# Memory keys and values from float32 weights as loaded, and no convolution chunk on TensorE

## The chip, the cores and the metric

One core of a Trainium2 chip runs the whole program. The metric is device time in microseconds (us) of one execution. Engines are called as the profile calls them: PE (TensorE; PEld is its weight load), DVE (VectorE), ACT (ScalarE), POOL (GpSimd), SP (SyncE, whose queue issues nearly all DMAs here). Each engine takes its instructions in an order that the program's scheduler fixed when the kernel was built.

## What is computed

One decoding step of a two-layer decoder for 512 prompt tokens and 64 sample tokens (8 sequences of 8), model width 1024. Layer 0 mixes tokens with a conformer convolution, layer 1 with causal pooling; each layer then has cross-attention into 256 memory tokens and a gated feed-forward part. The parts that the change touches:

```python
def _mem_kv(mem, g_mem, w_kv):          # for each layer: mem [256, 1024], w_kv [1024, 2048]
    kv = (_rmsnorm(mem, g_mem) @ w_kv).reshape(b, N_MEM, 2, N_MEM_HEADS, MEM_HEAD_DIM)
    return kv[:, :, 0], kv[:, :, 1]

def _conformer_conv(h, prefix, ...):
    u = h @ w_in + b_in                 # [1024, 2048]
    a, gate = jnp.split(u, 2, axis=-1)
    glu = a * jax.nn.sigmoid(gate)
    c = _causal_dwconv(concat(prefix, glu), w_dw, b_dw)      # 31 taps, each channel by itself
    c = silu(layernorm(c, ln_g, ln_b))
    return c @ w_out + b_out
```

The keys and values of the memory are outputs, and the attention of their layer reads them. All products are wanted in float32 precision.

## The kernel before, in words

**Products.** A float32 product is made of three float16 products: both operands are split into hi and lo halves (`cp`, L137, on ACT writes hi; `lo`, L140, on DVE writes the rest), and hi·hi, hi·lo and lo·hi are added in PSUM by `mm` (L130). Turning goes through `tr` (L134), a PE transpose.

**Weight stream.** `build_units` lists all weights in the order of use, as units of 1 MB. SP loads each half (512 KB, L217 in `emit_dma`) into one of three raw buffers; `convert_next` splits the half into a slot (8 KB a partition; there are nine). `pump(n)` starts up to n further units if a slot is free; `get` starts units until the one asked for is there; `drop` frees a slot. A slot goes to the unit that was written next in the program, first freed first used, and the unit's conversion waits until the slot's earlier content has been read.

**Layer 0's mixer** (`conv_module`). Eight `pair(p)` steps, one for each 128 channels, multiply the normed tokens by `a_w_in` (24 products of 512 columns and 24 of 64 for each of gate and value); ACT evaluates them (L766 to L769), DVE multiplies (L770, L771). The 31-tap convolution of a chunk of channels follows as soon as its pair is done, with a lowered priority: by `PLAN`, chunks 0 and 2 (after pair 2), 4 (after pair 4), 5 and 6 (after pair 7) run on DVE as 31 steps each that add into PSUM (L657, L661); chunks 1 and 3 run on ACT (products) and POOL (sums, L676); chunk 7 runs on PE (`conv_pe`) as 93 products with diagonal matrices that `diag_build` makes on POOL (L725). The convolution of the sample tokens is shared by DVE (L689), ACT and POOL (`prefix_s`, `fresh_s`). Results lie in `CT`.

**Memory keys and values.** `mem_load` loads the 256 memory tokens. For each layer `mem_norm` normalises them (with the layer's gain row, a broadcast DMA, L280) and `mem_turn` turns and splits them, in pairs 2 to 4. `kv_part(l, n)`, eight in all, then multiplies them by a [1024, 512] piece of `c_w_kv`, which is two units: 2 x 24 products of 512 columns, evaluated by ACT and written out twice by SP (L594 to the output, L596 to a scratch from which attention loads them). After each part `pump(2)` starts two units. Units of layer 1's parts 1 to 3 are held back until convolution chunk 6 is done (`after`, L225).

**Then** the layer norm of the convolution (`ln_a`: PE turns, statistics on DVE L855, result on ACT L860; `ln_b`: turn back, ACT L874, split), first for token tiles 0 and 1, interleaved with the last parts; then the product with `a_w_out` (`natural_stage`), which in program order comes after all eight parts; then attention.

Of the kernel before, what the change touches and what calls it, by code (L numbers as in the profile page):

```python
# [14 lines left out]
D = 1024  # L15
# [31 lines left out]
class Step:  # L47
    """The whole inference step. On-chip data live in one SBUF tile cut by hand; the products are exact
    16-bit splits (hi + lo) of both operands, scaled by powers of two, accumulated in float32."""

    def __init__(self, tc, ctx, ins, outs):
# [25 lines left out]
        self.PA0 = take(288)  # L77
# [7 lines left out]
        self.after = {}  # L85
        self.free = deque(range(self.NSLOT))
# [7 lines left out]
    # ---- views  # L94
# [29 lines left out]
    def release(self, s):  # L124
        if s < 100:
            self.free.append(s)

    # ---- engine helpers
# [13 lines left out]
    # ---- weight stream  # L142
    def build_units(self):
# [60 lines left out]
        self.rawat = {}  # L204
        self.special = {("down", 0): None}

    def emit_dma(self, upto):
        while self.n_dma < min(upto, 2 * len(self.units)):
            u, half = divmod(self.n_dma, 2)
            r = self.rawq()  # L210
            src = self.units[u][1][half]
            dst = self.f(self.RAW0 + r * 1024, 1024)
# [5 lines left out]
            self.rawat[self.n_dma] = r  # L218
# [38 lines left out]
    def pump(self, n=1):  # L257
        while n > 0 and self.n_cv < len(self.units):
            key = self.units[self.n_cv][0]
            if not self.free and not (self.lent and key[0] in ("K", "V") and key[2] in self.lent_to):  # L260
# [14 lines left out]
    # ---- norms  # L275
# [29 lines left out]
    def split_T(self, h0, P, hi, lo):  # L305
        """h0 [P tokens, 1024] -> hi/lo views [128, 8, P] of its transpose."""
# [9 lines left out]
    def split_D(self, src, o, dst):  # L316
        """src [128 tokens, 1024] -> hi/lo views [128, 8, 128] of its transpose, turned on the way by the DMA."""
# [57 lines left out]
    def nat_prompt(self, acc, act, woff, nk, hook=None):  # L375
        """acc [128, 1024] = act^T . 64 w;  act(k, s) the stationary [128, 128]."""
# [14 lines left out]
    def nat_last(self, acc, act, woff, nk, half):  # L391
        """nat_prompt by halves of the output's columns, with half(n) after each."""
# [10 lines left out]
    def nat_sample(self, acc, act, woff, nk, order=None, hooks=None):  # L403
        """acc rows 0..63: hi part, rows 64..127: lo part of the 64 sample tokens."""
# [12 lines left out]
    def fold(self, acc, tmp, out):  # L417
        """out[0:64] = acc[0:64] + acc[64:128]"""
# [36 lines left out]
    # ---- start  # L455
    def start(self):
# [8 lines left out]
        # parameters, one row per channel chunk, to be turned  # L465
# [8 lines left out]
        for i in range(2):  # L474
            later(self.f(so + 128 * (1 + i), 128)[:124], wdw[i * 124:(i + 1) * 124])
            blocks.append((so + 128 * (1 + i), 124))
        blocks2 = []
# [54 lines left out]
        for bl, dst, n in ((blocks, self.PA0, 288), (blocks2, self.PF0, 352)):  # L532
# [14 lines left out]
    # ---- memory keys and values of the prompt  # L547
    def mem_load(self):
        self.ms, self.mt = self.slot(), self.slot()
# [4 lines left out]
    def mem_norm(self, l):  # L554
        """The normed memory of layer l, and what turns it."""
        mo, to = self.slot_off(self.ms), self.slot_off(self.mt)
        g = self.gain(self.A["norm_gains"][l, 6])
        for t in range(2):
            self.pre_norm(self.f(mo + t * D, D), 128, g, self.f(to + t * D, D))

    def mem_turn(self, l):
        to = self.slot_off(self.mt)
        s = self.slot()
        v = self.h(self.slot_off(s), 4096).rearrange("p (c s m) -> p c s m", c=8, s=2)
        for t in range(2):
            r = slice(t * 128, t * 128 + 128)
            self.split_T(self.f(to + t * D, D), 128, v[:, :, 0, r], v[:, :, 1, r])
        self.mts[l] = (s, v)
        if l == 1:
            self.release(self.ms)  # L570
            self.release(self.mt)

    def kv_part(self, l, n):
        nc = self.nc
        if (l, n) == (0, 0):
            self.kvs = self.slot()
# [1030 lines left out]
```

## Time and profile before

| | us |
|---|---|
| median of three timed runs | 1551.38 (1549.75 to 1552.37) |
| span of the profiled execution | 1546.2 |
| median less span | 5.2 |
| PE busy in the span | 1422.7 |
| DVE, ACT, POOL busy | 956.0, 778.1, 303.8 |

The span runs from the first to the last instruction of the profiled execution; what lies around it is taken as the 5.2 us to the median. A busy PE is not PE at its peak: its clock is granted in steps, shown as PEclk (1.00 is 2.4 GHz, 0.50 is 1.2 GHz).

### The profile page before, as it was taken

To read this page: it belongs to the slowest core of one execution; us is meant where nothing else is said; L and a number is where in the kernel's file an instruction comes from. 1 tells how busy PE (TensorE), PEld (TensorE's weight loads), DVE (VectorE), ACT (ScalarE), POOL (GpSimd) and SP (SyncE) were. 2 spreads that over 40 slices of the span, in tenths; PEclk is the share of its full clock that TensorE was granted. 3 is DMA by queue.
4 is the path that set the end of the run, shared out by engine and by line. 5 is a ranking of instruction groups with operands and counts; after the bars stand their busy time and mean duration, and the time that the engine had idled before them with its cause. 6 is when DMAs were issued, how large, how long until landed. Compare 5 with 4: busy or idle time off the path is not lost.

```text
span 1546.2 us, 25434 instructions
## 1 busy us (share of the span) xinstructions
PE 1422.7 (92%) x10298; PEld 775.7 (50%) x10298; DVE 956.0 (62%) x1166; ACT 778.1 (50%) x1278; POOL 303.8 (20%) x533
## 2 busy tenths in 40 slices
PE   6867888988888999999999999988999999999998
PEld 3433433434575565555554456657546555554443
DVE  4999996576468759555562236457977756564101
ACT  4867633764356658555551125346767546554000
POOL 4797950012000112000014010200112000000000
PEclk9988989999999999999999999899999999999999
DMA  8301357768996765233241105799795333232000
GB/s 277 129 28 41 113 156 224 250 186 156 242 249 202 195 187 153 69 111 94 77 125 55 55 1 137 173 206 240 231 234 183 94 105 100 68 113 71 22 19 21
DMA packets 208288, 208.50 MB, mean 135 GB/s; under 512 B 107726, under 2 KB 173822, under 8 KB 208147
## 3 DMA queue, kind: packets, MB, share of 16 engines
q1 hardware_dynamic: 208170, 206.88, 47.8%
q8 instruction: 80, 1.31, 0.4%
q14 instruction: 38, 0.30, 0.1%
HBM read 169.41 MB, written 13.22 MB: 118 GB/s over the span
## 4 chain that ended last, share of the span: by engine, by line
PE 61%; DMA 14%; DVE 13%; ACT 5%; issue 4%; POOL 2%; SPq 2%; DVEq 0%; POOLq 0%; ACTq 0%
PE psum L130 60%; DVE mem L140 4%; DVE psum L661 4%; ACT mem L137 3%; DMA mem<-in_c_w_kv_dram 3%; DMA mem<-in_a_w_in_dram 2%; DMA mem<-in_cache_mem_k_dram 1%; DMA mem<-in_c_w_q_dram 1%; DVE mem L689 1%; DMA mem<-mem 1%; DMA mem<-in_cache_mem_v_dram 1%; DMA mem<-in_c_w_o_dram 1%; SPq L322 1%; POOL mem L676 1%; ACT mem L1004 1%
## 5 line engine op out<-in xcount | busy, mean ns | idle before, releaser
L130 PE MATMUL psum<-mem 128*128 128x512 f16 (+4 forms) x9933 | 1383.5, 301 | 69.8 <-DVE mem L140 25.5
L130 PEld LDWEIGHTS <-mem 128*128 128x128 f16 x9789 | 715.8, 99 | 690.0 <-issue 82.1
L137 ACT ACTIVATE mem<-mem 128x1024 f16<-128x1024 f32 (+7 forms) x615 | 432.4, 744 | 376.7 <-DMA mem<-in_c_w_kv_dram 52.5
L140 DVE SCALAR_TENSOR_TENSOR mem<-mem 128x1024 f16<-128x1024 f32 (+2 forms) x377 | 375.2, 1020 | 150.3 <-ACT mem L137 149.6
L137 ACT ACTIVATE mem<-psum 128x512 f16<-128x512 f32 (+11 forms) x250 | 136.9, 570 | 170.2 <-PE psum L130 156.7
L1220 DVE SCALAR_TENSOR_TENSOR mem<-mem 128x592 f32<-128x592 f32 x176 | 137.2, 830 | 105.0 <-ACT mem L1216 104.8
L285 POOL TENSOR_SCALAR mem<-mem 128x1 f32<-128x1 f32 (+1 forms) x68 | 32.5, 478 | 471.4 <-ACT mem L293 304.4
L661 DVE SCALAR_TENSOR_TENSOR psum<-mem,psum 128x512 f32<-128x512 f32 x145 | 102.4, 745 | 0.7
L134 PE MATMUL psum<-mem 128*128 128x128 f32 (+7 forms) x365 | 57.0, 285 | 46.1 <-DVE mem L314 15.8
L1213 POOL COPY mem<-mem 128x32 f32<-128x32 f32 x44 | 13.3, 303 | 420.5 <-issue 373.3
L320 DVE TENSOR_TENSOR mem<-mem 128x1024 f16<-128x1024 f32 x48 | 58.3, 1222 | 57.6 <-ACT mem L137 42.6
L676 POOL TENSOR_TENSOR mem<-mem 128x512 f32<-128x512 f32 x60 | 89.4, 1494 | 9.6 <-ACT mem L137 8.4
L295 DVE SCALAR_TENSOR_TENSOR mem<-psum,mem 128x1024 f32<-128x1024 f32 x19 | 24.4, 1283 | 102.1 <-POOL mem L286 101.9
L134 PEld LDWEIGHTS psum<-mem 128*128 128x128 f32 (+7 forms) x365 | 42.2, 147 | 69.7 <-DVE mem L314 25.4
L1216 ACT ACTIVATE mem<-mem 128x592 f32<-128x592 f32 x88 | 73.0, 873 | 4.2 <-POOL mem L1213 0.4
L293 ACT ACTIVATE mem<-psum 128x1024 f32<-128x1024 f32 x19 | 19.3, 1017 | 96.4 <-PE psum L130 96.4
L140 DVE SCALAR_TENSOR_TENSOR mem<-psum,mem 128x512 f16<-128x512 f32 (+2 forms) x58 | 30.7, 545 | 52.4 <-ACT mem L137 52.4
L303 DVE SCALAR_TENSOR_TENSOR mem<-mem 128x1024 f32<-128x1024 f32 (+1 forms) x34 | 45.5, 1337 | 26.1 <-POOL mem L286 15.6
L301 ACT ACTIVATE mem<-mem 128x1024 f32<-128x1024 f32 (+1 forms) x34 | 35.7, 1051 | 32.1 <-DVE mem L296 28.7
L1225 ACT ACTIVATE mem<-mem 128x592 f32<-128x592 f32 x44 | 30.6, 695 | 40.4 <-DVE mem L1220 40.4
L286 POOL TENSOR_TENSOR mem<-mem 128x1 f32<-128x1 f32 (+1 forms) x68 | 38.3, 563 | 5.3
L696 POOL TENSOR_TENSOR mem<-mem 128x512 f32<-128x512 f32 (+7 forms) x29 | 38.6, 1330 | 3.3 <-DVE mem L689 2.4
(78 smaller groups left out, 437.9 us busy)
## 6 DMA issues: line engine op xcount, KB each, us to landing
mem<-in_f_w_up_dram SPq DMA_DIRECT2D x88, 512.0 KB
mem<-in_f_w_down_dram SPq DMA_DIRECT2D x44, 512.0 KB
mem<-in_c_w_kv_dram SPq DMA_DIRECT2D x32, 512.0 KB
mem<-in_cache_mem_k_dram SPq DMA_DIRECT2D x32, 512.0 KB
mem<-in_cache_mem_v_dram SPq DMA_DIRECT2D x32, 512.0 KB
mem<-in_a_w_in_dram SPq DMA_DIRECT2D x16, 512.0 KB
mem<-in_c_w_q_dram SPq DMA_DIRECT2D x16, 512.0 KB
mem<-in_c_w_o_dram SPq DMA_DIRECT2D x16, 512.0 KB
```

Of the source, the lines that this page charges most:

```text
L130: self.nc.tensor.matmul(out, a, b, start=start, stop=stop)
L134: self.nc.tensor.matmul(out, in_, self.ident[:P, :P], is_transpose=True, start=True, stop=True)
L137: self.nc.scalar.activation(out, in_, AF.Copy, scale=scale)
L140: self.nc.vector.scalar_tensor_tensor(out, src, scale, hi, op0=ALU.mult, op1=ALU.subtract)
L286: self.nc.gpsimd.tensor_tensor(r[:P], a[:P], self.mhalf[:P], op=ALU.pow)
L303: self.nc.vector.scalar_tensor_tensor(h0, x, r, g[:P], op0=ALU.mult, op1=ALU.mult)
L320: self.nc.vector.tensor_tensor(lo, src, hi, op=ALU.subtract)
L661: nc.vector.scalar_tensor_tensor(o, PE_[:, c, k:k + 512], self.w_dw(k, c), b, op0=ALU.mult, op1=ALU.add)
L676: nc.gpsimd.tensor_tensor(CT[:, c], CT[:, c], pr, op=ALU.add)
L696: nc.gpsimd.tensor_tensor(sv[:, :, :, :n], sv[:, :, :, :n], pr, op=ALU.add)
L1216: nc.scalar.activation(c[:, g], e[:, g, 2:594], AF.Identity, scale=self.fw(l, 2, ch), bias=self.fb(l, ch))
L1220: nc.vector.scalar_tensor_tensor(c[:, g], e[:, g, k:k + TAPN], self.fw(l, k, ch), c[:, g], op0=ALU.mult, op1=ALU.add)
```

## The change

Memory: the 256 tokens are turned once, without a norm, as float32 (`mem_turn` in pair 4); each layer's gain is multiplied in when DVE moves the turned tokens out of PSUM (8 operations of 128x512), and each token's 1/rms when ACT evaluates a part. The gains are loaded as two small rows with the parameters rather than as two broadcasts. Keys and values: `kv_part` multiplies float32 tokens by the float32 weights as they were loaded, 2 x 8 float32 products of 512 columns in place of 2 x 24 float16 ones; its units are not converted, and their halves go by DMA into the slot itself ("R"). Results rotate over four PSUM banks. Slots: the second memory slot and the slot of the diagonal matrices are not taken any more; after pair 7 the place of the normed tokens (`HT0`) serves as two more slots, for kv units alone. Convolution: chunk 7 goes to DVE; by `PLAN` DVE runs chunks 0 and 2 (after pair 2), 4 and 5 (after pair 5), 6 and 7 (after pair 7). The hold on layer 1's units is gone. The rest of the diff takes out comments.

```diff
 def slot(self, key=None):
+        if key and key[0] == "kv" and self.spare:
+            return self.spare.popleft()
 ...
 def kv(l, n):
-                               v[:, 4 * g + 2:4 * g + 4, n * 512:n * 512 + 512]], WS, None))
+                               v[:, 4 * g + 2:4 * g + 4, n * 512:n * 512 + 512]], 1.0, "R"))
 ...
 def emit_dma(self, upto):
+            if self.units[u][3] == "R":
+                if u not in self.direct:
+                    return
+                dst = self.f(self.direct[u] + half * 1024, 1024)
 ...
 def convert_next(self, off):
+        if kind == "R":
+            n = 2 * self.n_cv + 1
+            self.direct[self.n_cv] = off
+            self.emit_dma(n + 1)
+            self.emit_dma(n + 1 + self.ahead(n))
+            self.n_cv += 1
+            return key
 ...
+    def mem_turn(self):
+        nc = self.nc
+        mo = self.slot_off(self.ms)
+        self.kvs = self.slot()
         for t in range(2):
+            ms, a = self.sc(), self.sc()
+            nc.scalar.activation(self.f(self.slot_off(self.kvs) + t * D, D), self.f(mo + t * D, D), AF.Square,
+                                 scale=1.0 / 32, accum_out=ms)
+            nc.gpsimd.tensor_scalar(a, ms, 1.0, RMS_EPS, op0=ALU.mult, op1=ALU.add)
+            nc.gpsimd.tensor_tensor(self.mem_r(t), a, self.mhalf, op=ALU.pow)
+        for l in range(2):
+            s = self.slot()
+            self.mts[l] = (s, self.f(self.slot_off(s), 2048).rearrange("p (c m) -> p c m", c=8))
+        for q in range(4):
+            tb = self.bank(self.trb()).rearrange("p (c m) -> p c m", c=2)
+            for j in range(2):
+                for t in range(2):
+                    c = 2 * q + j
+                    self.tr(tb[:, j, t * 128:t * 128 + 128], self.f(mo + t * D + c * 128, 128))
+            for l in range(2):
+                g = self.f(self.PA0 + 288 + l * 8 + 2 * q, 2).unsqueeze(2).to_broadcast([128, 2, 256])
+                nc.vector.tensor_tensor(self.mts[l][1][:, 2 * q:2 * q + 2], tb, g, op=ALU.mult)
+        self.release(self.ms)
 ...
 def kv_part(self, l, n):
         for t in range(2):
-            acc = self.bank(2 + t)
+            acc = self.bank(self.kvb())
             for k in range(8):
-                off = self.get(("kv", l, n, k // 4))
-                wh = self.h(off + (k % 4) * 256, 512)
-                wl = self.h(off + 1024 + (k % 4) * 256, 512)
-                a = v[:, k, 0, t * 128:t * 128 + 128]
-                self.mm(acc, a, wh, k == 0, False)
-                self.mm(acc, a, wl, False, False)
-                a = v[:, k, 1, t * 128:t * 128 + 128]
-                self.mm(acc, a, wh, False, k == 7)
-            self.cp(o[:, t], acc, IWS)
+                w = self.f(self.get(("kv", l, n, k // 4)) + (k % 4) * 512, 512)
+                self.mm(acc, v[:, k, t * 128:t * 128 + 128], w, k == 0, k == 7)
+            self.cp(o[:, t], acc, self.mem_r(t))
 ...
-    PLAN = {1: (("p", 1),), 2: (("d", 0, 2),), 3: (("p", 3),), 4: (("d", 4),),
-            7: (("e", 7), ("d", 5, 6), ("s",))}
+    PLAN = {1: (("p", 1),), 2: (("d", 0, 2),), 3: (("p", 3),), 5: (("d", 4, 5),),
+            7: (("d", 6, 7), ("s",))}
 ...
         for p in range(2, 8):
             pair(p)
-            if p == 2:
-                self.mem_norm(0)
-            if p == 3:
-                self.mem_turn(0)
-                self.mem_norm(1)
             if p == 4:
-                self.mem_turn(1)
+                self.mem_turn()
             self.pump(1)
+        self.spares = (self.HT0, self.HT0 + 2048)
+        self.spare.extend(self.spares)
 ...
-        for n, g in self.KG:
-            self.after[("kv", 1, n, g)] = CT[:, self.KGC, 511:512]
```

## Rows read from the trace of the kernel before

**Rows 1.** The page: busy time, then 40 slices (38.7 us each) in tenths.

```profile
PE 1422.7 (92%) x10298; PEld 775.7 (50%) x10298; DVE 956.0 (62%) x1166; ACT 778.1 (50%) x1278; POOL 303.8 (20%) x533
PE   6867888988888999999999999988999999999998
DVE  4999996576468759555562236457977756564101
PEclk9988989999999999999999999899999999999999
DMA  8301357768996765233241105799795333232000
```

**Rows 2.** Busy time by stretch: length, PE, PEld, DVE, ACT, POOL (count); clock, DMA, GB/s.

```profile
60.00:165.00 105.00, 76.89 (x585) 40.23 (x584) 103.61 (x133) 76.73 (x199) 92.98 (x72) 0.87 0.15 46
165.00:258.00 93.00, 77.31 (x349) 34.66 (x348) 85.33 (x97) 38.20 (x56) 49.74 (x47) 0.94 0.51 163
258.00:305.00 47.00, 42.36 (x204) 20.55 (x204) 25.07 (x30) 29.43 (x38) 5.81 (x8) 0.96 0.74 235
305.00:345.00 40.00, 32.67 (x156) 15.58 (x155) 30.48 (x34) 27.35 (x40) 6.63 (x13) 0.96 0.68 209
...
136.00:150.00 14.00, 6.15 (x24) 2.69 (x24) 14.00 (x19) 6.83 (x15) 10.95 (x10) 0.51 0.31 89
```

**Rows 3.** The chain of waits from 140 to 345 us: shares by line.

```profile
by line: DMA mem<-in_c_w_kv_dram 22.3%; DVE mem L140 15.9%; issue 9.7%; ACT mem L137 9.2%; DVE psum L661 7.7%; POOL mem L676 6.8%; PE psum L130 5.8%; DMA mem<-in_c_w_q_dram 5.5%; DMA mem<-in_a_w_out_dram 3.1%; DMA out_dram<-mem 2.7%; DVE me
```

**Rows 4.** Timeline: PE's last pair products, DVE's last convolution step, PE's first `a_w_out` products.

```profile
159.72 2.60 PE L130 MATMUL psum<-mem 128*128 128x64 f16 x45
...
256.39 0.75 DVE L661 SCALAR_TENSOR_TENSOR mem<-mem,psum 128x512 f32<-128x512 f32 x1
...
305.56 2.76 PE L130 MATMUL psum<-mem 128*128 128x512 f16 x12
```

**Rows 5.** PE products: a timeline row, then a group by form (858.9 to 861.2 us).

```profile
309.18 6.85 PE L130 MATMUL psum<-mem 128*128 128x512 f16 x31
...
L130 PE MATMUL psum<-mem 128*128 128x128 f32 x16 | 1.9, 275 | 0.0
```

**Rows 6.** Waits (total us, times, longest): PE 29 to 165, SP 60 to 165, ACT 165 to 305.

```profile
PE psum L134 <- DVE mem L314: 14.9, 4, 9.5
PE psum L130 <- ACT mem L137: 4.2, 1, 4.2
...
SPq L280 <- DVE mem L303: 46.6, 2, 41.5
...
ACT mem L137 <- DMA mem<-in_c_w_kv_dram: 46.1, 19, 11.2
...
ACT mem L137 <- POOL mem L225: 8.3, 1, 8.3
```

**Rows 7.** Groups by line and form, DVE: 60 to 165, then 165 to 258, then 258 to 335.

```profile
L140 DVE SCALAR_TENSOR_TENSOR mem<-mem 128x1024 f16<-128x1024 f32 x8 | 13.2, 1663 | 1.3 <-ACT mem L137 1.3
L303 DVE SCALAR_TENSOR_TENSOR mem<-mem 128x1024 f32<-128x1024 f32 x3 | 5.8, 1922 | 0.0
L314 DVE TENSOR_TENSOR mem<-psum,mem 128x512 f16<-128x512 f32 x7 | 4.7, 678 | 0.0
...
L661 DVE SCALAR_TENSOR_TENSOR psum<-mem,psum 128x512 f32<-128x512 f32 x69 | 48.0, 746 | 0.4
L140 DVE SCALAR_TENSOR_TENSOR mem<-mem 128x1024 f16<-128x1024 f32 x18 | 34.4, 1922 | 6.5 <-ACT mem L137 6.5
...
L140 DVE SCALAR_TENSOR_TENSOR mem<-mem 128x1024 f16<-128x1024 f32 x27 | 32.7, 1216 | 25.3 <-ACT mem L137 25.2
```

**Rows 8.** Timeline: a kv half's issue and first use; chain of waits: a kv load.

```profile
199.43 0.39 SPq L217 DMA_DIRECT2D mem<-in_c_w_kv_dram  x1
...
203.25 1.06 ACT L137 ACTIVATE mem<-mem 128x1024 f16<-128x1024 f32 x1 [11.21 <-DMA mem<-in_c_w_kv_dram]
...
276.81 9.27 DMA mem<-in_c_w_kv_dram
```

More of the change, by code (lines that the diff above doesn't have):

```diff
@@ L76, in __init__ @@
         self.ID0 = take(128)
-        self.PA0 = take(288)
+        self.PA0 = take(304)
         self.PF0 = take(352)
@@ L126, in release @@
             self.free.append(s)
+        elif s in self.spares:
+            self.spare.append(s)
     def mm(self, out, a, b, start, stop):
@@ L204, in build_units @@
         self.rawat = {}
+        self.direct = {}
         self.special = {("down", 0): None}
@@ L209, in emit_dma @@
             u, half = divmod(self.n_dma, 2)
-            r = self.rawq()
             src = self.units[u][1][half]
-            dst = self.f(self.RAW0 + r * 1024, 1024)
+            if self.units[u][3] == "R":
+                if u not in self.direct:
+                    return
+                dst = self.f(self.direct[u] + half * 1024, 1024)
+            else:
+                self.rawat[self.n_dma] = self.rawq()
+                dst = self.f(self.RAW0 + self.rawat[self.n_dma] * 1024, 1024)
             if len(src.shape) == 3:
@@ L259, in pump @@
             key = self.units[self.n_cv][0]
-            if not self.free and not (self.lent and key[0] in ("K", "V") and key[2] in self.lent_to):
+            if not self.free and not (key[0] == "kv" and self.spare) and not (self.lent and key[0] in ("K", "V") and key[2] in self.lent_to):
                 return
@@ L476, in start @@
             blocks.append((so + 128 * (1 + i), 124))
+        for l in range(2):
+            later(self.f(so + 1920, 128)[l * 8:l * 8 + 8], A["norm_gains"][l, 6].rearrange("(c p) -> c p", p=128))
+        blocks.append((so + 1920, 16))
         blocks2 = []
@@ L531, in start @@
             fin(t)
-        for bl, dst, n in ((blocks, self.PA0, 288), (blocks2, self.PF0, 352)):
+        for bl, dst, n in ((blocks, self.PA0, 304), (blocks2, self.PF0, 352)):
             tb = self.bank(self.trb())
@@ L548, in mem_load @@
     def mem_load(self):
-        self.ms, self.mt = self.slot(), self.slot()
+        self.ms = self.slot()
         mo = self.slot_off(self.ms)
@@ L552, in mem_load, with mem_r @@
             self.nc.sync.dma_start(self.f(mo + t * D, D), self.A["mem_prompt"][0, t * 128:(t + 1) * 128, :])
-    def mem_norm(self, l):
-        mo, to = self.slot_off(self.ms), self.slot_off(self.mt)
-        g = self.gain(self.A["norm_gains"][l, 6])
+    def mem_turn(self):
+        nc = self.nc
+        mo = self.slot_off(self.ms)
+        self.kvs = self.slot()
         for t in range(2):
[L559 to L571, printed above, removed]
+            ms, a = self.sc(), self.sc()
[12 more added lines that the diff above has]
+                    self.tr(tb[:, j, t * 128:t * 128 + 128], self.f(mo + t * D + c * 128, 128))
+            for l in range(2):
+                g = self.f(self.PA0 + 288 + l * 8 + 2 * q, 2).unsqueeze(2).to_broadcast([128, 2, 256])
+                nc.vector.tensor_tensor(self.mts[l][1][:, 2 * q:2 * q + 2], tb, g, op=ALU.mult)
+        self.release(self.ms)
+    def mem_r(self, t):
+        return self.f(self.SM0 + 90 + t, 1)
     def kv_part(self, l, n):
         nc = self.nc
-        if (l, n) == (0, 0):
-            self.kvs = self.slot()
         s, v = self.mts[l]
@@ L705, in fresh_s @@
                 e.tensor_tensor(sv[:, :, :, n:], sv[:, :, :, n:], pr, op=ALU.add)
-        wsp = self.h(self.G0 + 11888, 496).rearrange("p (s k c) -> p s k c", s=2, k=CW)
-        idh = self.h(self.G0 + 12136, 128)
-        wall = self.f(self.PA0 + 40, 248).rearrange("p (k c) -> p k c", k=CW)
-        self.cp(idh, self.ident)
-        self.cp(wsp[:, 0], wall, WS)
-        self.lo(wsp[:, 1], wall, wsp[:, 0], WS)
-        diag = {}
-        def diag_build(c):
-            ds = self.slot()
-            parts = [self.h(self.slot_off(ds), 4096), CT[:, 5:8].rearrange("p c n -> p (c n)").bitcast(F16),
-                     self.h(self.G0 + 12200, 768)]
-            for i, (k0, k1) in enumerate(((0, 16), (16, 28), (28, 31))):
-                v = parts[i][:, :(k1 - k0) * 256].rearrange("p (s k n) -> p s k n", s=2, n=128)
-                for sp in range(2):
-                    for k in range(k0, k1, self.DK):
-                        n = min(self.DK, k1 - k)
-                        nc.gpsimd.tensor_tensor(v[:, sp, k - k0:k - k0 + n], idh.unsqueeze(1).to_broadcast([128, n, 128]),
-                                                wsp[:, sp, k:k + n, c].unsqueeze(2).to_broadcast([128, n, 128]),
-                                                op=ALU.mult)
-                for k in range(k0, k1):
-                    diag[k] = (v[:, 0, k - k0], v[:, 1, k - k0])
-            diag["slot"] = ds
-        def conv_pe(c):
-            xs = self.h(self.T0, 1084).rearrange("p (s n) -> p s n", s=2)
-            self.cp(xs[:, 0], PE_[:, c])
-            nc.vector.tensor_tensor(xs[:, 1], PE_[:, c], xs[:, 0], op=ALU.subtract)
-            acc = self.bank(0)
-            for k in range(CW):
-                dh, dl = diag[k]
-                self.mm(acc, dh, xs[:, 0, k:k + 512], k == 0, False)
-                self.mm(acc, dh, xs[:, 1, k:k + 512], False, False)
-                self.mm(acc, dl, xs[:, 0, k:k + 512], False, k == CW - 1)
-            nc.scalar.activation(CT[:, c], acc, AF.Identity, scale=IWS, bias=self.b_dw(c))
-            self.release(diag["slot"])
-        KIND = {"d": lambda *c: conv_dve(c), "p": conv_pool, "s": fresh_s, "e": conv_pe}
+        KIND = {"d": lambda *c: conv_dve(c), "p": conv_pool, "s": fresh_s}
         def pair(p):
@@ L790, in conv_module @@
         self.pump(2)
-        diag_build(7)
         state_turn()
@@ L888, in conv_module @@
             kv_next()
+        assert len(self.spare) == 2
+        self.spare.clear()
+        self.spares = ()
         offs = {j: self.get(("aout", j)) for j in range(4)}
```

3 lines of the change are left out of this document (2 added, 1 removed).

## The prediction

> **What bounds the kernel now.** Read the page's slices first [rows 1]: in slices 1 to 9 (to about 345 us) the engines change roles, and from about slice 14 on PE is at 9 tenths nearly throughout. The change touches the first region alone, so what it is worth is decided there. The view by stretches [rows 2] splits it. From 60 to 165 us, the eight pairs, DVE is busy 103.6 of 105 us, DMA is at 0.15, and PE is busy 76.9 us at a clock of 0.87. From 165 to 305 us, the eight kv parts, PE is busy 77.3 + 42.4 = 119.7 of 140 us, DVE and DMA are part busy, and the chain of waits [rows 3] names the loads of `c_w_kv` first (22%) and the splitting on DVE next (16%): the stream load, hi on ACT, lo on DVE, product sets the pace. Three times mark the region [rows 4]: the last pair product ends at 159.72 + 2.60 = 162.3 us, the convolution at 256.39 + 0.75 = 257.1 us, and the first product with `a_w_out` starts at 305.6 us. All that comes after hangs on that start, so I forecast how far it moves and carry that to the end.
>
> **Price of the products.** A run of 31 float16 products of 512 columns takes 6.85 us, with about 0.38 us of it the length of a single one that is not yet overlapped: (6.85 - 0.38) / 30 = 0.216 us each [rows 5]. The kv products cost 8 x 48 x 0.216 = 83 us, the chunk on PE 93 x 0.216 = 20 us. A float32 product of that size is not in the trace; the nearest rows are float32 products of 128 columns in the pooling mixer: 8 of them (one token tile, eight chunks) stand as 16 records, two each, 1.9 us in all with a mean of 0.275: (1.9 - 0.275) / 15 = 0.108 us a record [rows 5]. If the price goes by columns, 512 cost 4 x 2 x 0.108 = 0.87 us, and 8 x 16 x 0.87 = 111 us. Bounds: if the whole 1.9 us scales, 4 x 1.9 / 8 = 0.95 us and 122 us; if a record ran at the float16 pace, 2 x 0.216 and 55 us. I take 111, because the float16 pace itself goes by columns. So PE gets 111 - 83 - 20 = 8 us more work, and 16 transposes less (about 2 us).
>
> The Trainium skill (TensorE: Matmul & The Clock Gate, Back-to-back issue gap) gives about 131 ns for a product of 512 columns in a sustained stream. That speaks against the change: what goes would be 477 x 0.131 = 62 us, and PE would gain 49 us of work instead of 8. The trace disagrees, with 216 ns in a long run [rows 5], so the row decides.
>
> **Pairs, 60 to 165 us.** (a) PE waits 14.9 us, in four waits, for DVE to take turned memory out of the one PSUM bank that serves (L314) [rows 6]. Eight such groups become four, each to be emptied by two DVE operations, and none waits for a norm. I keep 5 us: -10. (b) PE waits 4.2 us for the hi half of the last `a` unit [rows 6], whose slot is that of the memory tokens, read by the last memory norm; now it takes a slot that has been free since pair 3: -4. (c) From 136 to 150 us, behind such waits, the clock is 0.51 [rows 2], and 0.87 over 105 us is a loss of 13.7 us; with half the waits gone I take half: -7. (d) DVE loses two kinds of work here: 3 of the 8 lo operations at 1.66 us (the kv ones) and the memory norms, 3 x 1.92; the 7 subtractions at 0.68 are matched by 8 multiplications of the same size, which I price alike [rows 7]. That is 11 us, which convolution steps fill. (e) SP's queue stood 41.5 us behind a gain row that waited for the last memory norm (L280) [rows 6]; the kv loads queued behind it. Without memory gains both layer gains find free buffers, so kv loads can start as soon as slots do; instead SP holds a kv load until the memory is turned, with only further loads behind it. Added small loads are two of 4 KB each, two broadcasts of 512 KB go: nothing taken. The last pair product ends at 162.3 - 21 = 141 us. Bounds: no gain, since convolution steps keep DVE just as busy and pair work may queue behind them (162), to all of (a) to (c), -33 (129).
>
> **Convolution.** DVE up to 257 us loses the 18 kv lo operations (34.4 us), the 3 of (d) (5.0), four memory norms (three of them 5.8, so 7.7) and gains chunk 7, 31 x 48.0/69 = 21.6 us [rows 7]. With the waits for ACT (6.5) that is 257 - 54 + 22 = 225 us. The lo operations cost 1.92 us here and 1.22 after 258 us [rows 7]; at the lower price less goes, 18 x 0.7 = 13 us, which with some waiting for pairs gives the upper bound. Bounds: 215 to 245. POOL ends 21 us earlier without `diag_build`, which nobody waits for.
>
> **Parts, from 141 us.** Products 111; turning for the layer norm and the state output 7 (some 60 transposes at 0.11). Loads: 16 MB in 111 us is 151 GB/s, less than the 235 of 258 to 305 us [rows 2]. But a unit now goes straight into a slot and can start only when that slot's last product is done. By the order of freeing, of 16 units only three (second units of parts 2, 4 and 6, counted from 0) get a slot that the part just before still reads to its end. Such a load has 4 products, 3.5 us, of cover; a lone half took 203.25 - 199.43 = 3.8 us, a load in a full queue 9.3 us [rows 8]. Between 0.3 and 6 us each; I take 2, near the lone one, because the other units are already in: 6 us. ACT's evaluation and four banks hide. What goes: 46.1 us of ACT waiting for kv loads and 8.3 for the hold (L225) [rows 6]. The layer norm begins at 225 us, in the middle of the parts; before it took 257 to 306 us, interleaved with loads and parts; 225 + 49 = 274 is no later than PE by much, and I take 5 us of waiting of PE for it (0 to 20). So the start is 141 + 111 + 7 + 6 + 5 = 270, against 305.6: -35.6.
>
> **After it.** The `a_w_out` and `c_w_q` weights follow kv in the stream; on the chain they are 3.1% and 5.5% of 205 us [rows 3], 18 us. The kv units no longer pass the raw buffers, so these can be loaded and split under the parts. PE is idle 7.3 of 40 us from 305 to 345 [rows 2]; I take 3 us (0 to 7). Later stages keep their work; a changed order there is worth ±3. Sum: 1546.2 - 35.6 - 3 = 1507.6 us of span, plus 5.2 to the median: 1513.
>
> **Rivals.**
> 1. The layer norm sets the start. If DVE finishes at 240 and the norm takes its 49 us as before, the start is at 289: -17, and 1546.2 - 17 - 3 + 5.2 = 1531. For: it alternates between PE and three others, and PE's fixed order may set it behind long float32 parts. Against: ACT and DVE have nothing else then.
> 2. The pairs don't get shorter, because DVE has as much low-priority work queued as before: start at 291, -15, and 1533.
> 3. Slower: slots. If each of the eight parts, not three, meets a load that starts at its beginning, each takes 9.3 - 3.5 = 5.8 us, 46 us; with pairs at 162 the start is 162 + 111 + 7 + 46 + 5 = 331, +25, and 1576 us; with pairs at 141 it is 310, +4 us, and 1553 (1555.4 - 3). It decides from 40 us of load waits on (with pairs shortened), or 20 (without). For: three raw buffers ran ahead before, and no unit does now. Against: three units by count, and DMA has room.
> 4. More than forecast. Parts fill the gaps of the pairs, since nothing on ACT or DVE precedes them, and attention starts with its weights ready: start 255, -51 - 7, 1493.
> 5. The change doesn't do what it says: float32 products at the 55 us bound would make the convolution and the norm the limit, 225 + 30 = 255, and 1499. It lies with rival 4.
>
> **How the numbers follow.** Forecast 0.55 (its own range 1502 to 1526), rivals 1 and 2 together 0.24, 4 and 5 0.08, 3 with its two prices 0.13, of which 0.04 within 0.2% of no change. Leaving out the most of 3 and the outer part of 4, the range is 1496 to 1541. A measurement of this kernel can tell 0.2%, 3.1 us, from no change. Faster 0.87 (forecast and rivals 1, 2, 4 and 5), same 0.04 and slower 0.09 (rival 3).
>
> **What would show it.** In the changed profile: float32 products of 512 columns in 256 records spaced 0.43 us; the last pair product near 141 us with a clock above 0.9 in that stretch; no L280 wait of tens of us; DVE's last L661 near 225 us; the evaluations of the parts 14 us apart, three of the gaps by 0.3 to 6 us longer; the first `a_w_out` product near 270 us, and the same distance from there to the end as before, less 3. It is wrong if records are spaced otherwise, if PE idles more than 15 us between parts, or if the gain at that start is lost again in attention, where DMA is at 8 to 9 tenths in slices 10 to 12 [rows 1].

## The result, and the profile after

| | before | after |
|---|---|---|
| median, us | 1551.02 (4 runs, 1549.75 to 1552.37) | 1534.87 (4 runs, 1523.61 to 1538.13) |
| ratio | | 0.9884, 95% interval 0.9849 to 0.9919 |
| profiled execution: span, us | 1546.2 | 1533.0 (that run took 1534.7) |
| last pair product ends, us | 162.3 | 142.0 |
| convolution ends, us | 257.1 | 255.8 |
| first `a_w_out` product, us | 305.6 | 283.9 |

The change is faster by 16 us, inside the range of 1496 to 1541, but 22 us short of the forecast of 1513. The page of the changed kernel, busy times and slices [rows 1]:

```profile
PE 1424.6 (93%) x10062; PEld 778.8 (51%) x10062; DVE 929.1 (61%) x1159; ACT 741.8 (48%) x1230; POOL 265.9 (17%) x507
PE   6979779988898899999999999988999999999998
DVE  4899996465387857655651338357886756554101
PEclk9989989999999999999999999899999999999999
```

PE is as busy as before (1424.6 against 1422.7 us), so what was gained is idle time of PE. PE's third and fourth slices (77 to 153 us, the pairs and the first of the kv parts) rise from 6 and 7 to 7 and 9; the fifth and sixth (kv parts) fall from 8 to 7. The same by stretches [rows 2] (columns as there):

```profile
60.00:165.00 105.00, 95.53 (x642) 48.97 (x640) 103.30 (x146) 73.78 (x196) 92.82 (x79) 0.95 0.31 97
165.00:258.00 93.00, 74.03 (x177) 32.77 (x176) 89.38 (x100) 28.98 (x40) 40.86 (x32) 0.91 0.66 219
258.00:305.00 47.00, 43.78 (x170) 21.39 (x170) 16.21 (x26) 20.06 (x27) 4.59 (x10) 0.93 0.42 131
```

From 60 to 165 us PE gains 18.6 us of busy time, partly because the kv parts now begin at 142 us, inside this stretch, and the clock goes from 0.87 to 0.95 (0.94 up to 142 us, the pairs alone). From 165 to 258 us, where the parts should follow without a break, PE is idle 19 of 93 us. The timeline of PE there, and DVE's last convolution step [rows 4, 5]:

```profile
139.75 2.37 PE L135 MATMUL psum<-mem 128*128 128x512 f16 x18
142.39 10.46 PE L135 MATMUL psum<-mem 128*128 128x512 f32 x24
...
153.38 8.75 PE L135 MATMUL psum<-mem 128*128 128x512 f32 x20
...
198.27 9.75 PE L135 MATMUL psum<-mem 128*128 128x512 f32 x18 [17.24 <-DMA mem<-in_c_w_kv_dram]
209.75 10.57 PE L135 MATMUL psum<-mem 128*128 128x512 f32 x24 [1.73 <-DMA mem<-in_c_w_kv_dram]
...
255.01 0.75 DVE L684 SCALAR_TENSOR_TENSOR mem<-mem,psum 128x512 f32<-128x512 f32 x1
...
283.88 3.51 PE L135 MATMUL psum<-mem 128*128 128x512 f16 x8
```

One gap of 17.24 us stands in the middle of the parts. Behind it PE runs with no further gap over 2 us to 277 us, although the convolution ends at 255.8. Why the load that ends the gap came so late is seen on SP and DVE (timeline, then what SP waited for from 160 to 200 us and PE from 142 to 285 us: total, times, longest):

```profile
161.87 0.38 SPq L229 DMA_DIRECT2D mem<-in_c_w_kv_dram  x1
...
180.72 12.23 SPq L229 DMA_DIRECT2D mem<-in_a_w_out_dram  x3
193.05 0.90 SPq L229 DMA_DIRECT2D mem<-in_c_w_kv_dram  x2
...
165.82 14.87 DVE L145 SCALAR_TENSOR_TENSOR mem<-mem 128x1024 f16<-128x1024 f32 x1
...
SPq L229 <- DVE mem L145: 26.6, 3, 15.6
...
PE psum L135 <- DMA mem<-in_c_w_kv_dram: 19.0, 2, 17.2
```

Three loads of `a_w_out` halves stand in SP's order ahead of two kv loads. Each needs a raw buffer, which is free when DVE has split the half that lies in it, and the first of these splits took 14.87 us, with a usual price of 1.22 us [rows 7]. So no kv load was issued from 162 to 193 us, although DMA had room: its busy share there was 0.26.

### The profile page after: what moved, and what is told of

Same layout as the page of the kernel before. It is cut to its first block, busy times and chain, and to the rows that moved or that the text cites. A ratio compares the mean times of both kernels' runs of the same rounds, so it can differ in the third digit from the quotient of the medians.

```text
span 1533.0 us, 24832 instructions
## 1 busy us (share of the span) xinstructions
PE 1424.6 (93%) x10062; PEld 778.8 (51%) x10062; DVE 929.1 (61%) x1159; ACT 741.8 (48%) x1230; POOL 265.9 (17%) x507
## 5 line engine op out<-in xcount | busy, mean ns | idle before, releaser
L135 PE MATMUL psum<-mem 128*128 128x512 f16 (+7 forms) x9712 | 1386.5, 304 | 68.6 <-DMA mem<-in_c_w_kv_dram 19.0
L135 PEld LDWEIGHTS <-mem 128*128 128x128 f16 x9312 | 670.0, 99 | 614.0 <-issue 53.7
L142 ACT ACTIVATE mem<-mem 128x1024 f16<-128x1024 f32 (+8 forms) x580 | 397.1, 729 | 343.0 <-PE psum L135 52.1
L145 DVE SCALAR_TENSOR_TENSOR mem<-mem 128x1024 f16<-128x1024 f32 (+3 forms) x344 | 335.6, 1000 | 147.7 <-ACT mem L142 138.2
L142 ACT ACTIVATE mem<-psum 128x512 f16<-128x512 f32 (+9 forms) x226 | 123.4, 570 | 175.2 <-PE psum L135 169.4
L684 DVE SCALAR_TENSOR_TENSOR psum<-mem,psum 128x512 f32<-128x512 f32 x174 | 121.9, 747 | 0.9
L303 POOL TENSOR_SCALAR mem<-mem 128x1 f32<-128x1 f32 (+1 forms) x64 | 23.7, 371 | 507.8 <-ACT mem L311 298.8
L135 PEld LDWEIGHTS psum<-mem 128*128 128x128 f32 (+2 forms) x400 | 69.5, 202 | 81.1 <-issue 56.9
L699 POOL TENSOR_TENSOR mem<-mem 128x512 f32<-128x512 f32 x60 | 82.5, 1378 | 6.7 <-ACT mem L142 5.5
L145 DVE SCALAR_TENSOR_TENSOR mem<-psum,mem 128x512 f16<-128x512 f32 (+2 forms) x58 | 30.7, 547 | 57.3 <-ACT mem L142 57.3
L321 DVE SCALAR_TENSOR_TENSOR mem<-mem 128x1024 f32<-128x1024 f32 (+1 forms) x30 | 38.4, 1282 | 27.6 <-POOL mem L304 20.1
```

The source lines that it names most:

```text
L135: self.nc.tensor.matmul(out, a, b, start=start, stop=stop)
L142: self.nc.scalar.activation(out, in_, AF.Copy, scale=scale)
L145: self.nc.vector.scalar_tensor_tensor(out, src, scale, hi, op0=ALU.mult, op1=ALU.subtract)
L321: self.nc.vector.scalar_tensor_tensor(h0, x, r, g[:P], op0=ALU.mult, op1=ALU.mult)
L684: nc.vector.scalar_tensor_tensor(o, PE_[:, c, k:k + 512], self.w_dw(k, c), b, op0=ALU.mult, op1=ALU.add)
L699: nc.gpsimd.tensor_tensor(CT[:, c], CT[:, c], pr, op=ALU.add)
```

## The experiments

Theory A: the shortfall is this gap, made by `a_w_out` units that come ahead of kv units in SP's order. Theory B: it is the convolution's end, which 12 splits of `a_w_out` and `c_w_q` delay. All runs in one table. "kv waits" is the time that PE stood for kv loads from 142 us to the first `a_w_out` product ("start"); "split" is the longest lo operation of DVE on 128x1024 (L145; L140 in `conv_alone`) between 150 and 200 us. The columns from "split" on are read from the profiled execution; times in us.

| run | median (range) | ratio to before (95%) | profiled run | split | kv waits | conv. ends | start |
|---|---|---|---|---|---|---|---|
| after | 1534.9 (1523.6–1538.1) | 0.988 (0.985–0.992) | 1534.7 | 14.87 | 19.0 | 255.8 | 283.9 |
| after_again | 1535.5 (1519.7–1537.9) | 0.990 (0.987–0.994) | 1519.7 | 2.08 | 3.6 | 242.1 | 270.1 |
| after_third | one run | | 1523.8 | 2.08 | 4.7 | 242.4 | 269.7 |
| kv_alone | 1549.3 (1538.6–1561.6) | 1.001 (0.997–1.004) | 1549.0 | 1.73 | 7.7 | 208.3 | 295.5 |
| conv_alone | 1573.8 (1569.7–1578.0) | 1.015 (1.012–1.019) | 1575.1 | 4.53 | none | 296.0 | 322.7 |
| hold_aout | 1529.8 (1524.5–1541.6) | 0.988 (0.983–0.993) | 1524.5 | 1.21 | 6.8 | 241.9 | 270.9 |
| hold_to_conv_end | 1534.7 (1532.8–1536.3) | 0.991 (0.990–0.993) | 1532.8 | 14.21 | 10.7 | 239.0 | 283.6 |
| fresh_dve | 1530.0 (1528.0–1532.3) | 0.987 (0.985–0.989) | 1532.3 | 2.28 | 11.7 | 255.9 | 282.7 |
| kv_loads_on_act | 1530.1 (1520.9–1533.8) | 0.987 (0.985–0.990) | 1527.5 | 14.87 | 13.6 | 255.2 | 281.6 |
| no_spare_slots | 1517.5 (1513.7–1519.1) | 0.980 (0.978–0.982) | 1513.7 | none | 3.0 | 227.1 | 265.2 |
| one_spare_slot | 1526.1 (1525.1–1527.4) | 0.984 (0.981–0.986) | 1526.4 | none | 3.2 | 241.1 | 275.2 |
| kv_alone_no_spare | 1538.9 (1538.2–1541.9) | 0.992 (0.989–0.995) | 1539.6 | none | 5.6 | 206.0 | 292.3 |
| turn_apart | 1522.3 (1518.1–1524.6) | 0.981 (0.978–0.983) | 1519.2 | none | 9.5 | 223.7 | 272.1 |

### The two parts alone

`kv_alone` has the new keys and values and the convolution of before (chunk 7 on PE); `conv_alone` is the kernel before with only the new `PLAN` and no `conv_pe`.

```diff
 kv_alone, against the kernel after:
+    PLAN = {1: (("p", 1),), 2: (("d", 0, 2),), 3: (("p", 3),), 4: (("d", 4),),
+            7: (("e", 7), ("d", 5, 6), ("s",))}
 ... (diag_build and conv_pe as before)
+        diag_build(7)
 conv_alone, against the kernel before:
+    PLAN = {1: (("p", 1),), 2: (("d", 0, 2),), 3: (("p", 3),), 5: (("d", 4, 5),),
+            7: (("d", 6, 7), ("s",))}
 ...
-        diag_build(7)
```

> The changed kernel with the convolution as before: chunk 7 on TensorE as 93 products, its matrices built on POOL in a slot, chunk 4 after pair 4, chunks 5 and 6 after pair 7. What is left of the change are the memory and kv parts. If the two parts of the change add up and chunk 7's 21.6 us on DVE are what it costs, the convolution ends about 22 us earlier than the 255.8 of the changed kernel, at 230 to 238, PE has 20 us more of products, and the start of a_w_out is 280 to 290: time 1530 to 1542, about the changed kernel's. If the move to DVE is what spoils the gain (DVE as the bound), the time is 1515 to 1525. If the move is what makes the gain, 1545 or more.

> The kernel before with the convolution as in the change: chunk 7 on DVE, chunks 4 and 5 after pair 5, 6 and 7 after pair 7, no products and no matrices for it. Memory and kv parts as before, with the hold of layer 1's units on chunk 6. DVE gets 21.6 us more before its last step (257.1 us), and layer 1's parts are held until then: convolution ends 275 to 282, start of a_w_out 15 to 25 us later than the 305.6 of before, time 1562 to 1576. If DVE had that much room, the time is within 5 us of 1551.

Measured: no change, and 24 us slower; together they are 16 us faster. Alone, the kv part is held by PE up to the start: DVE's last convolution step ends at 208 us, PE is busy 140.2 of 149.5 us from 146 to 295.5, and has kv products to 295.3. Its start is still 10 us earlier than before (305.6). The span is not shorter (1547.3 against 1546.2 us), so these 10 us are lost again behind the start; what loses them was not found, and the ten runs lie far apart. I had given a convolution that ends at 230 to 238 us and, for parts that add up, 1530 to 1542. Alone, the convolution part is held by DVE, whose last step ends 14 us later than I gave at most: PE's timeline in it, and its waits from 142 to 300 us:

```profile
258.76 0.90 PE L134 MATMUL psum<-mem 128*128 128x128 f32 x3 [19.38 <-DVE mem L661]
...
PE psum L134 <- DVE mem L661: 19.4, 1, 19.4
PE psum L130 <- DVE mem L140: 14.3, 3, 9.0
```

So the parts don't add: each takes work off the engine that the other one loads (chunk 7 off PE, the kv splits off DVE).

### Splits held back

```diff
+        for j in range(4):
+            self.after[("aout", j)] = CT[:, 6, 511:512]      # hold_aout; CT[:, 7, 511:512] in hold_to_conv_end
         parts = deque((a, n) for a in range(2) for n in range(4))
```

> The changed kernel with one edit: the four a_w_out units are not split before the last step of convolution chunk 6 (the hold that the kernel before had on kv units, now on these). Theory A: in the changed kernel the first product with a_w_out starts at 283.9 us because one split of a_w_out on DVE took 14.87 us (165.8 to 180.7) while POOL ran its sums, SP stood in front of the a_w_out load that needs the raw buffer freed by it, and two kv loads stood behind on SP, so PE idled 17.2 us up to 198 us; and because splits of a_w_out and c_w_q, 31 us in all, ran ahead of convolution steps, which end at 255.8. With the hold no wait of PE over 8 us before 260, convolution ends 225 to 235, start of a_w_out 262 to 268, time 16 to 22 us below the changed kernel's median: 1513 to 1520. Theory B: the start is set by the layer norm behind the parts and these splits only move; then they come after the convolution, the start stays at 280 or later, time 1532 or more.

> The changed kernel with the four a_w_out units (and with them, by the stream's order, all of c_w_q) held until the last convolution chunk, 7, is done; in the earlier run with the hold on chunk 6, 12 splits of 1.22 us and 4 us of waits stood between chunk 6 (done at 210 us) and the end of chunk 7 (241.9 us). Both theories: the convolution ends at 222 to 228 us. Theory A (products of the parts bound the stretch once the gap is gone): the first a_w_out product starts at 264 to 272 us, as with the other hold (270.9), median within 5 us of it, 1523 to 1534. Theory B (the convolution's end sets the start): 16 to 19 us earlier than with the other hold, at 252 to 256 us, median 1508 to 1518. If the units now come too late for the a_w_out products, the start is later than 272 us and PE waits there for DVE's splits.

In `hold_aout` no long split and no wait for a kv load over 2.1 us is left in the profiled run, and the start is at 270.9, what was forecast for the change. That run is the fastest of four that reach to 1541.6, and their median, 1529.8, is above the 1513 to 1520 that I gave. The convolution ends at 241.9 us, later than I gave, since 11 splits still come between chunk 6 (done at 210 us) and the end of chunk 7. For `hold_to_conv_end` the hold was a leaky tool: it stops only the first half of a unit, and one second half still came through, in `hold_aout` in 1.21 us, in `hold_to_conv_end` in 14.21. Behind the second, a gap of 6.5 us came back; PE waited 4.1 us more for kv loads that stood behind `c_w_q` in SP's order, and 4.2 for a convolution chunk that the layer norm turns (L684); and the start was at 283.6. Theory B falls with this pair: the convolution ended 2.9 us earlier than in `hold_aout`, and the start came 12.8 us later.

### The split and the queue

`fresh_dve` moves the products and sums of the sample tokens (`fresh_s`), which POOL does from 154 to 178 us, to DVE; `kv_loads_on_act` issues the kv loads from ACT.

```diff
 fresh_dve:
-    FRESH_DVE = False
+    FRESH_DVE = True
 kv_loads_on_act:
-            self.nc.sync.dma_start(dst, src)
+            q = self.nc.scalar if self.units[u][3] == "R" else self.nc.sync
+            q.dma_start(dst, src)
```

> The changed kernel with one edit: the 16 operations of fresh_s (new rows of the sample convolution) run on DVE instead of POOL, so that POOL's run of sums has gaps, since what is left there waits for ACT's products. Theory A1 (the split of 14.87 us waits because POOL goes from one operation to the next without a gap, and PE's wait of 17.2 us hangs on it): no split over 4 us, PE's wait for kv loads before 200 us under 6 us, convolution ends 245 to 253 (splits still ahead of it, 16 operations more on DVE, some 8 us), start of a_w_out 268 to 276, time 1519 to 1528. Theory A2 (SP's order alone: the a_w_out load stands ahead of kv loads, whatever the split takes): PE's wait stays at 10 us or more and the time within 4 us of 1535.

> The changed kernel with the loads of the kv units issued by ACT's queue in place of SP's, so that no kv load stands behind an a_w_out load in SP's order; the splits of a_w_out stay ahead of the convolution. Theory A (the 17.2 us gap of PE up to 198 us, made by the order in SP's queue, is what the forecast of 270 us missed): the gap is below 7 us, the convolution still ends at 253 to 258 us, and the first a_w_out product starts at 267 to 275 us, median 1519 to 1530. Theory B (the late end of the convolution sets the start): the convolution ends at 253 to 258 us and the start stays at 281 to 286 us, median 1532 to 1538. Third case: ACT stands at a kv load that waits for its slot, and pair or part evaluations behind it come late: PE gaps at evaluations of over 5 us, median above 1540.

Neither frees the start. In `fresh_dve` no split is long (2.28 us at most), but with 16 more operations DVE comes to the first one at 174.7 us only, SP issues the three `a_w_out` loads from 176.4 on and the next kv load at 188.1, and PE stands 9.7 us. In `kv_loads_on_act` the queue in front of the loads only changed its engine (ACT and PE timelines):

```profile
183.91 1.06 ACT L142 ACTIVATE mem<-mem 128x1024 f16<-128x1024 f32 x1 [10.78 <-DMA mem<-in_a_w_out_dram]
184.04 0.93 ACTq L230 DMA_DIRECT2D mem<-in_c_w_kv_dram  x2
...
189.56 13.24 PE L135 MATMUL psum<-mem 128*128 128x512 f32 x24 [9.58 <-DMA mem<-in_c_w_kv_dram]
```

ACT waits for an `a_w_out` half whose load waits for DVE's split of 14.87 us, and the kv loads stand behind ACT's wait. I expected this run to close the gap; it shows instead that the gap follows the kv loads to a second queue in which they stand behind an `a_w_out` conversion.

### The extra slots

```diff
 no_spare_slots, and kv_alone_no_spare (on kv_alone):
-        self.spares = (self.HT0, self.HT0 + 2048)
-        self.spare.extend(self.spares)
 ...
-        assert len(self.spare) == 2
 one_spare_slot:
+        self.spares = (self.HT0,)
```

> The changed kernel without the two extra slots in the place of the normed tokens. If slots bound the loads of the parts, as rival 3 of the prediction has it: a part's loads start only when the part before has been multiplied, 3 to 6 us in each of six parts or so, the start of a_w_out 18 to 40 us later than in the changed kernel, median 1550 to 1575. If SP's order is what delays the loads and slots are not short: within 5 us of the changed kernel's 1535.

> The changed kernel with one extra slot for kv units in place of two. The run without any was at 1517.5 us, with a_w_out started at 265.2 us; there every kv load but three a_w_out halves stands ahead of the a_w_out loads in SP's order, while with two extra slots they alternate. If the extra slots cost time because they let a_w_out units into the order ahead of kv units, one slot alternates too, a little less early: PE gaps of 3 to 17 us at a kv load, start 268 to 283 us, median 1522 to 1534, between the two. If the extra slots cost nothing and the run without them was better for another reason (fewer splits before the end of the convolution alone): PE gaps below 3 us and a median within 3 us of 1517 or of 1535.

> The kernel with the new memory keys and values and the convolution as before (chunk 7 on TensorE), now without the two extra slots. With them it took 1549.3 us, level with the kernel before. If the extra slots were what ate the gain there too: the start of a_w_out moves to that of the run without extra slots, 265 us, plus the chunk on PE, 93 products of 0.216 us, 20 us: 285 (282 to 290), median 1534 to 1541. If PE's work alone held it at 1549: no change, 1546 to 1552, start 293 to 297 us.

Without the extra slots the kernel is faster than the kernel before and than the change, by 2.0% against before and 17 to 18 us below the median of the change; with one it lies between (there PE waits 3.6 us for ACT's evaluation of a part and 2.7 for a kv load, and behind the first wait the clock is 0.72 from 211.7 to 222.6 us); and the kv part alone takes 10 us less without them than with them. For the first I had given a loss or no difference, and a gain stood in no theory. SP's and PE's timeline of `no_spare_slots`, and its stretch from 165 to 262 us (columns as above):

```profile
160.55 2.34 SPq L229 DMA_DIRECT2D mem<-in_c_w_kv_dram  x3
166.20 5.52 SPq L229 DMA_DIRECT2D mem<-in_c_w_kv_dram  x4
182.93 6.39 SPq L229 DMA_DIRECT2D mem<-in_c_w_kv_dram  x6
198.75 6.31 SPq L229 DMA_DIRECT2D mem<-in_c_w_kv_dram  x7
211.78 2.42 SPq L229 DMA_DIRECT2D mem<-in_c_w_kv_dram  x2
222.34 9.67 SPq L229 DMA_DIRECT2D mem<-in_a_w_out_dram  x5
...
190.66 15.72 PE L135 MATMUL psum<-mem 128*128 128x512 f32 x36 [1.41 <-DMA mem<-in_c_w_kv_dram]
...
208.05 4.56 PE L135 MATMUL psum<-mem 128*128 128x512 f32 x10 [1.56 <-DMA mem<-in_c_w_kv_dram]
...
265.22 3.32 PE L135 MATMUL psum<-mem 128*128 128x512 f16 x8
...
165.00:262.00 97.00, 93.20 (x243) 42.62 (x241) 78.39 (x110) 41.53 (x53) 39.18 (x36) 1.00 0.79 260
```

With nine slots the kv units themselves fill them, and the last five `a_w_out` halves are issued only when all kv loads are (the first three lie in the raw buffers since about 90 us in either kernel). An extra slot taken by a kv unit leaves an ordinary one to the next unit of the stream, and that is `a_w_out`, which brings splits for DVE and a raw buffer to wait for. Here no split is done between 150 and 200 us, DVE ends the convolution at 227.1 (forecast: 225), and PE is busy 93.2 of the 97 us from 165 to 262 at a clock of 1.00. In `kv_alone_no_spare` the start comes 3 us earlier than with the slots, 292.3, not at the 285 that I gave; the other 6 us of the two profiled spans' difference lie spread over the later stages, so this run shows that the slots cost time there, and not that they do it in the same way. No run gives the kv units two slots in another place, so whether it is their number or their place (`HT0`, free only after pair 7) stays open.

### The same program twice more

> The changed kernel once more, on the same chip as the three others, with a second profile. If the 5 us that the first profile lost again after the start of a_w_out (in layer 1's attention, 134.2 us from its first softmax to the first up product against 132.3 before) belong to the kernel, this stage is 134 to 135 us again; if they are variation between executions, it differs by 2 us or more in either direction (it was 131.4 to 140.0 in the runs so far). Gap of PE 16 to 18 us ending near 198 us, first a_w_out product 282 to 286 us, median 1530 to 1538 by either.

> A third look at the changed kernel. Two profiled executions of it differed: in one a split of a_w_out took 14.87 us beside POOL's sums, PE stood 17.2 us up to 198 us, a_w_out started at 283.9 us and the run took 1534.7; in the other the same split took 1.84 us, PE stood 3.1 us, the start was 270.1 us and the run took 1519.7. If it is this split that parts the runs: either over 10 us, start 281 to 286, time 1533 to 1539, or under 3 us, start 268 to 272, time 1518 to 1525. A run of 1533 or more with a short split, or the reverse, would say that something else parts them.

DVE, SP and PE timelines of `after_again`:

```profile
166.47 1.84 DVE L145 SCALAR_TENSOR_TENSOR mem<-mem 128x1024 f16<-128x1024 f32 x1
...
168.34 10.70 SPq L229 DMA_DIRECT2D mem<-in_a_w_out_dram  x3
179.14 0.90 SPq L229 DMA_DIRECT2D mem<-in_c_w_kv_dram  x2
...
184.74 10.97 PE L135 MATMUL psum<-mem 128*128 128x512 f32 x18 [3.06 <-DMA mem<-in_c_w_kv_dram]
...
270.09 1.90 PE L135 MATMUL psum<-mem 128*128 128x512 f16 x8
```

The order of instructions is that of `after`, the split takes 1.84 us instead of 14.87, the gap is 3.1 instead of 17.2, and the start is at 270.09: the 270 of the forecast. `after_third` shows the same once more. The eleven timed runs of this program fall into two groups, eight from 1534.1 to 1538.1 us and three from 1519.7 to 1523.8, none between; the three traces, one in the first group and two in the second, put the long split with the first and the short one with the second. The other eight runs have no trace.

### The turning apart

On top of `no_spare_slots`, the four quarters of `mem_turn` follow one each behind pairs 4 to 7.

```diff
 ... (the loop over the quarters in mem_turn becomes mem_quarter(q))
             if p == 4:
                 self.mem_turn()
+            if p >= 4:
+                self.mem_quarter(p - 4)
```

> The changed kernel without the two extra slots, and with the four quarters of the memory's turning set one behind each of pairs 4 to 7, in place of all four behind pair 4, where PE waited 5.6 and 1.1 us at 102 and 115 us for DVE to empty the one PSUM bank. If these waits are on the path, PE being busy from there to the start of a_w_out: 6.7 us of waits and some 3 us at half clock go, last pair product at 133 to 137 us (was 142), start at 256 to 260 us, median 1507 to 1512 against 1517.5. If DVE, busy 103 of 105 us there, only shifts the wait to the pairs: last pair product at 140 to 143, median within 3 us of 1517.5.

The waits for L597 go, but others take their place (7.5 us for ACT's evaluations of the pairs), and the pairs end at 140.4 us, not 133 to 137. The time, 1522.3, is no better than the 1517.5 without this edit: the gap comes back by another door (SP and PE timelines):

```profile
188.37 2.71 SPq L807 DMA_DIRECT2D out_dram<-mem  x8
191.17 3.22 SPq L229 DMA_DIRECT2D mem<-in_c_w_kv_dram  x5
...
198.50 12.17 PE L135 MATMUL psum<-mem 128*128 128x512 f32 x24 [9.36 <-DMA mem<-in_c_w_kv_dram]
```

Five kv loads stand behind the outputs of the carried state, which waited 6.7 us for ACT. It is the same order a third time, with an output in front.

## Why the prediction was right and wrong

**Right: the pairs.** The last pair product ended at 142.0 (forecast 141), the clock from 60 us to there was 0.94, and SP's wait for the gain row was gone. PE's waits at the turning are 6.1 us in place of 14.9, near the 5 that I kept.

**Right: the price of the products.** In a run without a break, 20 records take 8.75 us, of which the last one's length is 0.59: 0.429 us from one to the next, two records a product, 0.86 us. All 256 records took 113.5 us of PE (forecast 111), some of it at half clock.

**Wrong: the loads, 6 us.** This is the step that failed; a second term, below, failed with it. I counted what a kv load waits for in its slot, and not what stands ahead of it in SP's order. Step (e) said that behind a held load there are "only further loads", and the step on what follows took the early loading and splitting of `a_w_out` "under the parts" for pure gain. It is the other way round: an `a_w_out` load ahead of a kv load waits for DVE's split of the half before it, and 19.0 us of PE's time went there, not 6, plus the cost of a lower clock behind the gap (0.81 from 198 to 208 us: 18 records in 9.75 us, 0.54 each). PE idle for more than 15 us between parts was one of the signs of being wrong that I had named. In two other executions of the same program it was 3.6 and 4.7 us, and the start was where the forecast had it, at 270.1 and 269.7.

**Wrong, and without effect: the convolution.** It ended at 255.8, 31 us late. Twelve lo operations of `a_w_out` and `c_w_q` run ahead of its last steps, in 31.0 us (mean 2.6): 15 us at the usual price, 16 more in the execution with the long split. With neither, in `no_spare_slots`, it is 227. The three traces of the change can't tell whether it set the start, which comes 27 to 28 us behind the convolution's end in each. That it didn't is shown by PE, which stands only 3.2 us for the layer norm between the parts and the start, by `hold_to_conv_end`, and by `no_spare_slots`, where the convolution ended 15 us earlier than in `after_again` and the start came 5 us earlier. The 5 us for the layer norm held (waits of 1.9 and 1.3).

**Wrong: after the start, -3 us.** From the start to the end of the span it takes 1240.6 us before, and 1249.1, 1247.9 and 1252.4 in the three traces of the change: 8.5 us more in the profiled run, where I had 3 less. Two stretches hold most of it. From the start to ACT's first exponential of layer 0's attention it is 133.1 us before, and 137.2, 135.5 and 139.2 in the three traces; PE does 120.1 us of work there in the first of them, not 112.8, and in two of the three the first eight products take 3.5 us at a clock of 0.50, not 1.9. From layer 1's first exponential to the first SiLU of its feed-forward part it is 144.2 us before, and 148.2, 147.5 and 147.8. Behind that, the last 361 us are the same within 0.2 us in all four traces. I had allowed ±3 for such changes of order. The three traces agree on the second stretch, so for the change it is no scatter between executions (of before there is one trace). What makes either was not found.

**The sum, with the measured terms.** 1512.8, plus 13.9 (start at 283.9, not 270), plus 11.5 (rest of 1249.1, not 1240.6 - 3), less 3.5 (what lies around the span is 1.7 us in the run of the change, I took 5.2 from a median of another run) gives 1534.7, the profiled run's time. Of the miss of 22 us, the start makes 14 and the rest of the way 11, and the runs show a cause for the first alone.

**The rivals.** Rival 1 gave nearly the right time, 1531, by a cause that did not act. Rival 3, slots, has its sign turned: more slots for kv units cost time. Two sums there are a little off, without effect on the range: rival 5's start of 255 gives 1498, not 1499, and rival 3's 1576 leaves out the 3 us that its 1553 takes off. The forecast's start is what the change gives without its extra slots (265), or in the executions in which the split comes through (270).

## What to carry to other kernels

A unit that is made ready earlier than it is needed is not free: in a queue with a fixed order, its load and all that the load waits for (a raw buffer, another engine's conversion) stand in front of the loads that the bottleneck is waiting for. Before giving a stream more buffers, list what the stream will fetch with them and where these fetches come in the issuing queue. And when one program's runs fall into two groups, take a second trace before explaining the first.

## What the runs showed of the hardware

A DVE operation that reads two operands from SBUF can be kept out for as long as POOL runs its own two-operand operations without a pause: 14.87 us here, against 1.22 as a rule. POOL in `after` beside the split that began at 165.82, the first two and the last four of 16 sums and products; then POOL in `after_again`, beside the split at 166.47:

```profile
165.32 1.27 POOL L699 TENSOR_TENSOR mem<-mem 128x512 f32<-128x512 f32 x1
166.54 0.73 POOL L728 TENSOR_TENSOR mem<-mem 128x256 f32<-128x256 f32 x1
...
178.35 7.01 POOL L699 TENSOR_TENSOR mem<-mem 128x512 f32<-128x512 f32 x4
...
165.96 1.27 POOL L699 TENSOR_TENSOR mem<-mem 128x512 f32<-128x512 f32 x1
167.19 1.71 POOL L728 TENSOR_TENSOR mem<-mem 128x256 f32<-128x256 f32 x1
```

In both the split began 0.5 us after the start of one of POOL's sums. In the first POOL's next sum took its usual 0.73 us, and the split ended at 180.7, 1.1 us after POOL's first pause (0.08 us, at 179.6, inside the row of four sums); in the second the next sum took 1.71 us and the split 1.84. The other long splits end in the same way, 1.1 us after POOL's first pause of 0.08 us: at 180.5 in `kv_loads_on_act`, at 180.6 in `hold_to_conv_end`, and at 199.4 in the kernel before (9.65 us, from 189.75). Which of the two gets in between is not decided by the program, since the same program did both, and 14 us of the kernel's start hang on it. The convolution steps (L684), which read one operand from PSUM, keep their 0.66 us beside the same sums.

The Trainium skill (SBUF — State Buffer, Who interferes with whom) says that a DVE instruction with two SBUF inputs contends with a GpSimd instruction that reads SBUF, one with at most one SBUF input, outside the two-port modes, does not, and that the order of issue decides who blocks. The traces agree, with 14.87 against 1.84 us and 0.66 us unchanged; that the wait can outlast many POOL instructions, to their first pause, is what these rows add.
